# Turning the memory's keys and the compressed branch's weights in 32x32 blocks by way of DRAM

## The chip, the cores and the metric

The kernel runs on one core of one Trainium2 chip. The metric is the time of one execution on the device in microseconds, the median of several runs. A core has five engines with their own instruction queues: TensorE (PE in the profile, with its weight loads as PEld), VectorE (DVE), ScalarE (ACT), GpSimd (POOL) and SyncE (SP). Each queue is worked off in order, and engines wait for each other at semaphores. DMAs are issued from the queues of SP, ACT and POOL.

## The reference, cut to what matters

The kernel computes one decoder block for 512 tokens of width 2048 in float32: a mixer of two head groups (eight NSA heads and four gated linear attention heads), a cross-attention over 256 memory tokens, and a SwiGLU layer. Two places bear on the change.

Each NSA head adds three branches, each an attention over other keys and weighted by a gate. The compressed branch has 31 block keys and values:

```python
s = jnp.einsum('bkgtd,bknd->bkgtn', qb, kc).astype(f32)
...
p = jax.nn.softmax(s, axis=-1)
p = jnp.where(jnp.any(vis, axis=-1)[:, None], p, 0.0)
o_cmp = jnp.einsum('bkgtn,bknd->bkgtd', p.astype(vc.dtype), vc)
...
return gb[..., 0:1] * o_cmp + gb[..., 1:2] * o_slc + gb[..., 2:3] * o_win
```

The cross-attention's keys are made from the memory, normalized by head and scaled by a gain:

```python
ck = rms_norm((hm @ w_ck).reshape(B, M, MEM_HEADS, MEM_DH), g_ck)
s = jnp.einsum('bthd,bmhd->bhtm', cq, ck).astype(jnp.float32)
```

## The kernel before, in words

**Products.** A float32 operand is split into a high part (a ScalarE copy that rounds, line 196) and a rest (a VectorE subtraction, line 196). A product is three matmuls of 512 columns: high by high, high by rest, rest by high (`mm3`, all recorded at line 109). Weights arrive by SP's DMAs, are split into the tiles `wh` and `wl` (three buffers each) and used by `project` and `natural`.

**Order of the work.** The program writes most stages as generators ("flows"). After every few matmuls of a projection the main program calls `flows.tick()`, and each flow whose pause is over adds its next instructions; `yield 2` means a pause of two ticks. A planner then orders each engine's queue by the order of the program, by priorities given to loads, and by modelled durations, and it gives out the tiles' buffers. The order on each queue is fixed before the run.

**The memory's keys.** At the start, `natural`-like loops multiply the memory by `w_cv` and `w_ck`. The flow `mem_keys` computes the norms of the keys and multiplies them in (line 470), which gives two tiles `rows[i]` of 128 memory tokens by 512 (four heads of 128). After a pause of eight ticks, TensorE turns them in eight transposes (line 479) into a PSUM bank `t`, ScalarE scales them by the gain `g_ck` (line 481), and POOL writes them to DRAM (line 440). During the projection by `w_out`, at step m == 4, POOL loads them again (lines 1080 and 1081); at m == 8 they are split into `ckp`, a tile pair with 256 columns for each head.

**An NSA head** (`nsa_head`). The scores of the first branch (selected blocks, with the compressed block scores beside them in the same bank) come first, then `weigh_blocks`: the softmax of the compressed branch in `pc` (128 tokens x 4 token tiles x 32 blocks), and at line 939 its product with the gate's coefficient, written three times side by side into `pc3`. Then come the second branch's scores (window). Later the weights are turned: four transposes of 128x96 (line 982) give `pct`, 96 rows by 512 tokens; ScalarE copies it to `pcs` (line 984) and VectorE replaces rows 64 to 95 by the rests (line 985). For each of the two branches, `turn(j)` transposes the weights (line 994) and splits them, and `weigh(j)` multiplies them by the values into the bank `o`. The first matmul into `o` is the compressed one (`vc` by `pcs`), two ticks after its operand's copy and subtraction. In `vc` rows 0 to 31 are the high part of the compressed values, rows 32 to 63 the rest and rows 64 to 95 the high part again, so that one matmul does all three products. Heads overlap: while one head turns and weighs, the next one computes its scores, and the following projection's matmuls lie between them.

**POOL's queue** also carries sums of later weights made in DRAM (`add_quarters` and `add_block`, lines 154, 156, 169 and 173), each issued after a given matmul; the loads and spills of the gates' rows (lines 1035 and 440, in `swish_gate`, whose product at line 1042 reads the load); and the loads of the mixer's rows (line 1063).

## Time and profile before

| | us |
|---|---|
| median of 3 runs | 2263.38 |
| lowest and highest | 2262.79, 2263.79 |
| the profiled execution | 2262.66 |
| its span, first to last instruction | 2260.9 |
| PE busy | 2252.3 |
| VectorE busy | 1681.7 |
| ScalarE busy | 1154.9 |
| POOL busy | 257.6 |

The profile is of one execution. A group's row gives line, engine, operation, the tile written and those read, the shape, how often, busy time and the mean duration. In a list by time, each row has its start, its length, how many instructions are merged in it, and in brackets how long the engine idled before it and what ended that. Matmuls are pipelined: one starts before the last one has ended, so their durations overlap, and what a matmul costs is the distance between starts. The granted TensorE clock is 1.00 throughout.

### The profile page before, as it was taken

To read this page: it belongs to the slowest core of one execution; us is meant where nothing else is said; L and a number is where in the kernel's file an instruction comes from. 1 tells how busy PE (TensorE), PEld (TensorE's weight loads), DVE (VectorE), ACT (ScalarE), POOL (GpSimd) and SP (SyncE) were. 2 spreads that over 40 slices of the span, in tenths; PEclk is the share of its full clock that TensorE was granted. 3 is DMA by queue.
4 is the path that set the end of the run, shared out by engine and by line. 5 is a ranking of instruction groups with operands and counts; after the bars stand their busy time and mean duration, and the time that the engine had idled before them with its cause. 6 is when DMAs were issued, how large, how long until landed. Compare 5 with 4: busy or idle time off the path is not lost.

```text
span 2260.9 us, 29119 instructions
## 1 busy us (share of the span) xinstructions
PE 2252.3 (100%) x10568; PEld 1871.4 (83%) x10568; DVE 1681.7 (74%) x2547; ACT 1154.9 (51%) x1712; POOL 257.6 (11%) x379
## 2 busy tenths in 40 slices
PE   9999999999999999999999999999999999999999
PEld 7898888888887888888888888888888888888787
DVE  7548876667778435587888888888888887766686
ACT  7534454556677224485455455545554554454443
POOL 0011121111112110020011101101110001001000
PEclk9999999999999999999999999999999999999999
DMA  8587667765558874196466555645564477768675
GB/s 302 176 211 182 166 180 218 208 179 132 163 158 242 219 192 126 56 253 231 140 186 191 167 163 187 192 158 172 190 201 139 155 272 265 266 240 274 244 271 182
DMA packets 129872, 443.59 MB, mean 196 GB/s; under 512 B 15328, under 2 KB 16736, under 8 KB 126784
## 3 DMA queue, kind: packets, MB, share of 16 engines
q1 hardware_dynamic: 83488, 308.97, 40.3%
q0 software_dynamic: 43792, 128.47, 23.5%
q10 hardware_dynamic: 2448, 4.28, 0.5%
q8 instruction: 83, 1.36, 0.2%
q14 instruction: 61, 0.50, 0.1%
HBM read 398.94 MB, written 105.64 MB: 223 GB/s over the span
## 4 chain that ended last, share of the span: by engine, by line
PE 95%; DVE 2%; DMA 2%; issue 1%; ACT 1%; SPq 0%; DVEq 0%; ACTq 0%
PE mm L109 51%; PE t L109 18%; PE s L109 14%; PE o L109 11%; DMA raw<-td 1%; PE t L994 1%; DVE ql L196 1%; DVE wl L196 0%; DMA HR<-h 0%; DMA on<-cmat 0%; DMA PH<-w_ck 0%; ACT wh L196 0%; DVE PB L196 0%; PE t L1151 0%; PE t L982 0%
## 5 line engine op out<-in xcount | busy, mean ns | idle before, releaser
L196 ACT CAST qh<-raw 128x1024 fp32r<-128x1024 f32 (+1 forms) x494 | 477.7, 976 | 453.5 <-PE o L109 131.6
L196 DVE TENSOR_TENSOR ql<-raw,qh 128x1024 fp32r<-128x1024 f32 (+1 forms) x494 | 549.4, 1122 | 81.3 <-PE t L109 25.7
L109 PE MATMUL mm<-X,wh 128*128 128x512 f32 x1664 | 524.1, 395 | 0.0
L109 PEld LDWEIGHTS mm<-X,wh 128*128 128x128 f32 x1664 | 305.7, 188 | 58.5 <-issue 0.8
L109 PE MATMUL t<-qh,PB 128*128 128x512 f32 x968 | 333.1, 389 | 0.0
L109 PE MATMUL mm<-X,wl 128*128 128x512 f32 x832 | 326.6, 393 | 0.2
L196 DVE TENSOR_TENSOR wl<-w,wh 128x1024 fp32r<-128x1024 f32 (+2 forms) x172 | 205.9, 1203 | 158.4 <-ACT wh L196 157.7
L196 ACT CAST wh<-w 128x1024 fp32r<-128x1024 f32 (+2 forms) x172 | 176.5, 1032 | 272.0 <-PE mm L109 181.5
L109 PE MATMUL mm<-qh,PB 128*128 128x512 f32 x868 | 309.3, 390 | 0.0
L109 PE MATMUL s<-qh,PB 128*128 128x512 f32 x672 | 231.1, 389 | 0.0
L109 PE MATMUL mm<-qh,PA 128*128 128x512 f32 x640 | 219.9, 389 | 0.0
L109 PEld LDWEIGHTS t<-qh,PB 128*128 128x128 f32 x968 | 181.7, 188 | 37.7
L109 PEld LDWEIGHTS mm<-qh,PB 128*128 128x128 f32 x868 | 163.0, 188 | 33.8 <-ACT qh L196 0.2
L109 PE MATMUL t<-ql,PB 128*128 128x512 f32 x484 | 188.4, 389 | 0.0
L109 PE MATMUL o<-qh,PB 128*128 128x512 f32 x484 | 187.6, 390 | 0.0
L109 PEld LDWEIGHTS mm<-X,wl 128*128 128x128 f32 x832 | 156.3, 188 | 34.2 <-DVE wl L196 1.7
L109 PE MATMUL mm<-ql,PB 128*128 128x512 f32 x434 | 169.6, 391 | 1.4 <-DVE ql L196 1.3
L109 PEld LDWEIGHTS s<-qh,PB 128*128 128x128 f32 x672 | 126.1, 188 | 25.7
L109 PEld LDWEIGHTS mm<-qh,PA 128*128 128x128 f32 x640 | 120.1, 188 | 24.9
L109 PE MATMUL s<-ql,PB 128*128 128x512 f32 x336 | 131.1, 390 | 0.1
L109 PE MATMUL mm<-ql,PA 128*128 128x512 f32 x320 | 124.6, 389 | 0.0
L1311 DVE TENSOR_TENSOR raw<-raw 128x1024 f32<-128x1024 f32 x80 | 96.9, 1221 | 16.2 <-DMA raw<-w_gu 15.9
(495 smaller groups left out, 3441.3 us busy)
## 6 DMA issues: line engine op xcount, KB each, us to landing
raw<-w_gu SPq DMA_DIRECT2D x80, 768.0 KB, 4.3
raw<-w_down SPq DMA_DIRECT2D x88, 512.0 KB, 5.1
raw<-w_gu SPq DMA_DIRECT2D x80, 512.0 KB, 3.6
td<-w_down POOLq DMA_DIRECT2D x66, 512.0 KB, 7.2
w<-w_a SPq DMA_DIRECT2D x60, 512.0 KB, 5.5
raw<-td SPq DMA_DIRECT2D x22, 1024.0 KB, 6.2
w<-w_out SPq DMA_DIRECT2D x32, 512.0 KB, 4.8
HR<-h POOLq DMA_DIRECT2D x28, 512.0 KB, 5.0
```

Of the source, the lines that this page charges most:

```text
L109: last_mm[0] = PE.matmul(*args, **kw)
L196: last_split[:] = S.copy(hi, src), V.tensor_sub(lo, src, hi)
L994: PE.transpose(tp[:, 128 * (i - j):128 * (i - j) + 128], ps_[b][:, POFF[i] + 128 * j:POFF[i] + 128 * j + 128], ident)
L1311: V.tensor_add(raw[:, 0:1024], raw[:, 0:1024], raw[:, 512:1536])
```

## The change

Both sets of transposes leave TensorE. VectorE turns each 32x32 block in place (`V.transpose`), and the blocks are put in order by the addresses of DMAs to DRAM and back.

The keys: each `rows[i]` is turned into `z`, and four POOL DMAs for each of the two tiles write it to DRAM so that the row is the head's dimension. The gain is applied after loading, at m == 8, by a ScalarE scaling whose input is a strided view; the splits write strided views of `ckp`. The pause of eight ticks becomes two, and there are two ticks after each tile.

The weights: `weigh_blocks` writes the product once into `pw` (128x128), turns it beside itself, writes it to DRAM by one POOL DMA and reads it back three times into `blocks` (96 rows, a buffer of the tag `e`). The copy and the subtraction read `blocks` through strided views, write `pcs` in a buffer of the tag `q1`, and stand with the compressed matmul in `weigh_compressed`, which is called in the second branch after `turn(0)` and its pause. The first matmul into `o` is now the first branch's.

```diff
-        yield 8
-        for a in range(2):
-            tp = bank("t")
-            for h in range(2):
-                for i in range(2):
-                    c = MEM * h + 128 * i
-                    PE.transpose(tp[:, c:c + 128], rows[i][:, 256 * a + 128 * h:256 * a + 128 * h + 128], ident)
-            ck = row("Q")
-            S.activation(ck, tp, AF.Copy, scale=vec("g_ck"))
-            memkv["k", a] = spill(ck)
-            yield 1
+        yield 2
+        for i, t in enumerate(rows):
+            z = row("Q")
+            V.transpose(view(z, 0, (32, 4), (128, 4), (1, 32)), t)
+            d = memkv["k", i] = dram.tile([128, 512], F32, name="ck", tag="ck", bufs=2)
+            for a in range(4):
+                G.dma_start(d[:, 128 * a:128 * a + 128].rearrange("(c s) x -> s c x", s=32),
+                            z[32 * a:32 * a + 32].rearrange("s (c x) -> s c x", x=128))
+            yield 2
...
-            V.tensor_mul(pc3, pc[:, :, None, :].to_broadcast([128, NT, 3, 32]),
-                         cf[:, 0, :][:, :, None, None].to_broadcast([128, NT, 3, 32]))
+            V.tensor_mul(pw[:, :128].rearrange("p (i n) -> p i n", n=32), pc,
+                         cf[:, 0, :][:, :, None].to_broadcast([128, NT, 32]))
+            V.transpose(pw[:, 128:], pw[:, :128])
+            d = dram.tile([128, 128], F32, name="pw", tag="pw", bufs=2)
+            G.dma_start(d, pw[:, 128:])
+            blocks = row("e")[:96]
+            for c in range(3):
+                G.dma_start(blocks[32 * c:32 * c + 32].rearrange("n (a x) -> n a x", x=128),
+                            d.rearrange("(a n) x -> n a x", n=32))
...
-        pct = bank("t")
-        for i in range(NT):
-            PE.transpose(pct[:96, 128 * i:128 * i + 128], pc3[:, i].rearrange("p r n -> p (r n)"), ident)
-        pcs = row("e", F32R)[:96]
-        S.copy(pcs, pct[:96])
-        V.tensor_sub(pcs[64:], pct[64:96], pcs[64:])
         o = None
+
+        def weigh_compressed():
+            pcs = row("q1", F32R)[:96]
+            new, old = [[view(t[a:], 0, *dims) for a in (0, 64)] for t, dims in
+                        ((pcs, ((32, 4), (128, 4), (1, 32))), (blocks, ((128, 4), (32, 4), (1, 32))))]
+            S.copy(new[0], old[0])
+            V.tensor_sub(new[1], old[1], new[1])
+            mm(o, vc[:, 128 * kv:128 * kv + 128], pcs, start=False, stop=False)
+
...
-                    start=False, stop=b == 1 and j == NT - 1)
+                    start=b == 0 and j == 0, stop=b == 1 and j == NT - 1)
...
             if b == 0:
                 o = bank("o")
-                mm(o, vc[:, 128 * kv:128 * kv + 128], pcs, start=True, stop=False)
+            else:
+                weigh_compressed()
...
         if m == 8:
             ckp = sb([128, 1280], "P", 2, F32R), sb([128, 1280], "P", 2, F32R)
-            for a in range(2):
-                split(*part(ckp, 512 * a, 512), ckt[a])
+            for i in range(2):
+                z = row("e")
+                S.activation(view(z, 0, (32, 4), (128, 4), (1, 32)), view(ckt[i], 0, (128, 4), (32, 4), (1, 32)),
+                             AF.Copy, scale=vec("g_ck"))
+                split(*[view(t, 128 * i, (256, 4), (1, 128)) for t in ckp], z.rearrange("p (h n) -> p h n", n=128))
```

## The prediction

> **What bounds the kernel now.** I read the page's busy times and its chain first.

> ```profile
> span 2260.9 us, 29119 instructions
> PE 2252.3 (100%) x10568; PEld 1871.4 (83%) x10568; DVE 1681.7 (74%) x2547; ACT 1154.9 (51%) x1712; POOL 257.6 (11%) x379
> PE 95%; DVE 2%; DMA 2%; issue 1%; ACT 1%; SPq 0%; DVEq 0%; ACTq 0%
> ```

> TensorE is busy for 2252.3 of 2260.9 us and carries 95% of the chain that ended last, so time taken off its queue is time off the end, as long as nothing makes it idle instead. A share over the whole span does not show that for the two stages that change, so next came the table by stretches of time (columns: sum of the stretch, busy PE, PEld, DVE, ACT, POOL with counts, granted clock, DMA share, GB/s). The memory's keys are turned near 62 us, the eight NSA heads run from 412 to 724 us, the turned keys are split between 750 and 800 us.

> ```profile
> 60.00:65.00 5.00, 4.98 (x26) 3.93 (x25) 5.00 (x11) 4.16 (x7) 0.54 (x1) 1.00 0.87 284
> 65.00:70.00 5.00, 5.00 (x23) 4.13 (x22) 4.89 (x9) 5.00 (x9) 0.54 (x1) 1.00 0.96 325
> 80.00:85.00 5.00, 5.00 (x23) 4.13 (x22) 1.82 (x2) 0.82 (x1) 0.00 (x0) 1.00 0.66 210
> 500.00:550.00 50.00, 50.00 (x265) 42.15 (x264) 35.56 (x101) 29.45 (x64) 7.90 (x10) 1.00 0.55 140
> 600.00:650.00 50.00, 50.00 (x267) 42.15 (x266) 36.26 (x108) 34.33 (x76) 8.04 (x11) 1.00 0.61 161
> 650.00:700.00 50.00, 49.66 (x261) 41.22 (x260) 41.08 (x121) 35.50 (x80) 9.69 (x15) 1.00 0.55 151
> 750.00:800.00 50.00, 50.00 (x222) 41.44 (x221) 17.33 (x19) 12.61 (x15) 7.36 (x9) 1.00 0.76 209
> ```

> TensorE has no idle time to give in the heads' stage, at full clock, and VectorE and ScalarE have some 9 us or more of 50 to spare. The list of PE's own waits from 380 to 760 us has one row:

> ```profile
> PE s L109 <- DVE mn L969: 0.3, 1, 0.3
> PEld s L109 <- DVE mn L969: 3.3, 12, 0.8
> ```

> (The second row is of the weight loads' own list, for the same hand-over; loads run ahead of the matmuls.) So both sets of transposes sit in a queue that is full of other matmuls (the next projection fills every gap), and they are paid in full.

> **What is removed.** 40 transposes: 32 of the weights (four for each head, line 982) and 8 of the keys (line 479). Their own rows, then how they stand in time, for head 0 and for the keys:

> ```profile
> L982 PE MATMUL t<-ident,pc x32: 270/273/282, 458.3 to 710.8; 128*96 128x128 f32 x32
> L479 PE MATMUL t<-ident,Q x8: 270/272/327, 62.1 to 64.5; 128*128 128x128 f32 x8
> ...
> 458.28 0.60 PE L982 MATMUL t<-ident,pc 128*96 128x128 f32 x4
> 458.71 0.60 PE L994 MATMUL t<-ident,P 128*128 128x128 f32 x4
> ...
> 62.07 0.83 PE L479 MATMUL t<-ident,Q 128*128 128x128 f32 x4
> 62.35 0.31 PEld L479 LDWEIGHTS t<-ident,Q 128*128 128x128 f32 x3 [0.37 <-DVE Q L470]
> 62.66 0.48 PE L109 MATMUL mm<-wh,X 128*128 128x512 f32 x1
> ```

> One transpose lasts 0.27 us, but four of them are done in 0.60, and the next group starts 0.43 us after the first: 458.71 - 458.28. That is 0.107 us each on the queue. The chain of waits says the same. Its shares for 400 to 725 us and for 55 to 70 us:

> ```profile
> by line: PE mm L109 64.7%; PE o L109 12.8%; PE s L109 11.9%; PE t L994 5.5%; PE t L109 3.8%; PE t L982 1.1%; DVE P L969 0.2%; PE t L831 0.1%; issue 0.0%; DVE mn L969 0.0%
> by line: PE mm L109 71.4%; PE o L109 22.7%; PE t L479 7.3%; issue 0.1%
> ```

> The heads' transposes: 1.1% of 325 us is 3.6 us, against 8 x 0.43 = 3.4 by the timeline; I take 3.5. The keys': 7.3% of 15 us is 1.1 us, with the 0.37 us in it for which the second weight load waited for VectorE's row; that wait goes with the transposes. Without it they are worth 0.7. Taken off: **3.5 + 1.1 = 4.6 us**, bounds 3.4 + 0.7 = 4.1 and 3.6 + 1.1 = 4.7.

> [...]

> **What is added or moved, and what hides it.** The rows that price it:

> ```profile
> L984 ACT CAST e<-t x8: 576/579/586, 458.9 to 711.4; 96x512 fp32r<-96x512 f32 x8
> L985 DVE TENSOR_TENSOR e<-t,e x8: 689/689/690, 459.5 to 712.2; 32x512 fp32r<-32x512 f32 x8
> L939 DVE TENSOR_TENSOR pc<-pc,cf x8: 549/550/559, 413.8 to 694.7; 128x384 f32<-128x384 f32 x8
> L935 DVE TENSOR_TENSOR pc<-pc,qs x8: 279/288/292, 412.0 to 690.7; 128x128 f32<-128x128 f32 x8
> L481 ACT ACTIVATE Q<-t,vecs x2: 674/677/680, 63.4 to 65.2; 128x512 f32<-128x512 f32 x2
> L1429 DVE STREAM_TRANSPOSE HR<-HR 128x512 f32<-128x512 f32 x16 | 10.5, 690 | 0.2 <-DMA HR<-x 0.2
> ```

> VectorE, heads: the product shrinks from 128x384 (0.55 us) to 128x128 (0.29), and a 128x128 turn comes in, a quarter of the 128x512 turn's 0.69, 0.17. The difference is under 0.1 us a head. VectorE, keys: two turns, 1.4 us, at 62 us, where it is full (5.00 of 5). What covers it: from 80 to 85 us VectorE works 1.82 of 5, and weight tiles are split three deep, so the 1.4 us are taken up before PE runs out of weights; without that cover they would cost 1.4. ScalarE: the two scalings of 0.68 leave that stage and come back between 750 and 800 us, where it works 12.61 of 50. The shorter pause of the key flow (2 ticks, not 8) moves work forward into VectorE's full stretch and nothing on PE. The product with the block values stays one 512-column matmul; it only moves to the second branch.

> The heads' ScalarE copy (L984) and VectorE subtraction (L985) stay, at 0.58 and 0.69 us if reading SBUF costs what reading PSUM did. But they move: before, two ticks of other matmuls lay between them and the product that reads them; now copy, subtraction and product stand together, and behind the product in the same PSUM bank wait the first value products of the second branch. **This is the unknown of the change.** Bounds a head: 0, if PE has other matmuls placed there, and 0.58 + 0.69 = 1.27, if it stands still for both; over eight heads 0 to 10.2 us. The nearest row is the hand-over of the scores' bank from VectorE to PE, which has no pause either: its weight loads waited twelve times, 3.3 us in all, and the matmuls for 0.3 us of that. Eight of twelve make 0.2 us, and I take that, near the lower end.

> The round trip through DRAM: POOL issues one write and three reads a head (32 more in all, of 64 KB), and eight writes for two with the keys (6 more). The reads wait on POOL for the write to land. Queued behind them on POOL: the sums in DRAM (L154, L156, L169, L173), the loads of the gates' rows (L1035), the spills. Rows for its length, head 2 and head 7:

> ```profile
> POOL gu L173 <- PE mm L109: 24.9, 3, 10.5
> gu<-w_gu POOLq DMA_DIRECT2D x8, 512.0 KB, 9.2
> x2r<-HR POOLq DMA_DIRECT2D x32, 128.0 KB, 2.6
> DMA to landing us min/median/max: 3.5/5.7/6.5
> ...
> 524.57 0.55 DVE L939 TENSOR_TENSOR pc<-pc,cf 128x384 f32<-128x384 f32 x1
> 559.28 0.48 PE L109 MATMUL o<-PH,KV 128*128 128x512 f32 x1
> 694.68 0.55 DVE L939 TENSOR_TENSOR pc<-pc,cf 128x384 f32<-128x384 f32 x1
> 719.75 0.50 PE L109 MATMUL o<-PH,KV 128*128 128x512 f32 x1
> ```

> The weights are made at 525.1 and 695.2; the first product that must come after them in the new place is at 559.3 and 719.7: 34 and 24.5 us of room. The trip takes 2 x 2.6 = 5.2 us at best, 2 x (9.2 + 10.5) = 39 at worst (two landings of the slowest kind, two sums waiting for PE ahead of it). By the nearest row, the 256 KB loads' 5.7 us, with one wait of 8, it is 19: hidden, cost 0.

> The sum: 4.6 - 0.2 = 4.4 us. The profiled execution took 2262.66 us around its span of 2260.9; the median of the three runs is 2263.38, 0.7 above. 2263.38 - 4.4 = **2259.0 us**, 0.19% less. About 0.2%, or 4.5 us, is what a measurement of this kernel can tell from no change, so the forecast lies on that edge.

> **The rivals.**

> *The transposes cost their duration.* 40 x 0.272 = 10.9 us go, or any part of the difference to 4.6 through freed PSUM banks: 2252.5 to 2258. For it: the duration rows. Against: the start times, and that PE waits for no bank now.

> *POOL's queue is held by the landings.* The tightest load behind it:

> ```profile
> 493.48 1.21 POOL L154 DMA_DIRECT2D td<-td  x1 [7.19 <-DMA w<-w_a]
> 494.22 1.08 POOL L1035 DMA_DIRECT2D st<-spill  x1
> L1042 DVE TENSOR_TENSOR st<-st,q x8: 679/691/692, 500.3 to 710.3; 128x512 f32<-128x512 f32 x8
> ```

> Issued at 494.2, landed 5.7 later, read at 500.3: 0.4 us to spare. Two landings, 11.4 us, less the 7.2 that POOL idles there anyway, make VectorE stand for up to 3.8 us, with PE's weights behind it; weights split ahead cover part of that. Half of that, at this gate and again at the last one, is 3.8 us lost: 2262.8. [...]

> *Another limit takes the gain.* The span stays, 2263.4. Against it: the 9 us and more that VectorE has free in each 50.

> *Slower: the product stands in PE's way.* The place is the second branch of every head, where PE's queue order is fixed before the run. If copy and subtraction come later than that order assumes, PE stops. From 4.5 / 8 = 0.56 us a head on, the gain is gone; at the full 1.27 it is 10.2 - 4.6 = 5.6 us slower, 2269.0. For it: no pause is left between them. Against it: the 0.3 us of PE's list.

> **How the numbers follow.** Forecast 0.62 (2257.5 to 2260.3), 0.29 below the 0.2% edge at 2258.85 and 0.33 above it; duration rival 0.09, faster; POOL 0.14 and another limit 0.05, no change; slower 0.10. Faster: 0.29 + 0.09 = 0.38. Same: 0.33 + 0.14 + 0.05 = 0.52. Slower: 0.10. The range leaves out most of the slower case and the deep part of the duration case: 2256.8 to 2263.4.

> **What would show it.** Lines 982 and 479 gone, PE's busy time down by 4 to 5 us, its head's period shorter by 0.43 us, and still no PE wait on the weights' tile in the heads' stage. Wrong it is if PE waits for ScalarE's or VectorE's part of the new product, if ScalarE waits for the read from DRAM, or if the gates' product waits for its load.

## The result, and the profile after

The changed kernel takes 2279.9 us (median of 6 runs, 2277.6 to 2282.9), the kernel before on the same chip 2263.1 (6 runs, 2262.3 to 2264.3): ratio 1.0073, 95% interval 1.0062 to 1.0083. By the ratio it is slower by 16.5 us (by the medians 16.8), where 4.4 us less were forecast. The profiled execution took 2281.3 us. All ratios here compare undisturbed executions; one execution of the run e7 below took 3516.3 us at a mean granted clock of 0.60 and is left out of its ratio.

The page of the kernel after, its busy times and its chain by line:

```profile
span 2279.5 us, 29129 instructions
PE 2254.8 (99%) x10528; PEld 1870.8 (82%) x10528; DVE 1683.0 (74%) x2557; ACT 1156.5 (51%) x1712; POOL 279.0 (12%) x417
PE mm L109 37%; PE t L109 15%; PE s L109 12%; PE o L109 8%; DMA e<-pw 1%; PE t L1004 1%; DMA st<-ck 0%; DMA raw<-gu 0%; DMA HR<-h 0%; ACT wh L196 0%; DVE ql L196 0%; DMA ss<-KV 0%; PE t L1165 0%; POOL e L946 0%; ACT e L1151 0%
```

The forty transposes are gone (10528 PE instructions instead of 10568), yet the span is 18.6 us longer and PE is busy 2.5 us *more*. The chain now runs through DMAs that were not on it before: `e<-pw`, the weights' read from DRAM, `st<-ck`, the keys' load (the kernel before loads them too, but off the chain), and through POOL's issue of the reads (`e L946`).

Where the time went is read from instructions that both kernels have. First the kernel before, from its lists by line (count, shortest, median and longest duration in ns, first and last start in us): the transposes of the compressed keys and values (the first ahead of the heads, the last in head 0) and those of the cross-attention; then the windows of the two stretches in question (columns as in the prediction).

```profile
L831 PE MATMUL t<-ident,q x4: 222/248/272, 362.2 to 454.6; 64*128 64x64 f32 x4
L1151 PE MATMUL t<-ident,e x32: 270/273/332, 907.9 to 954.8; 128*128 128x128 f32 x32
...
380.00:760.00 380.00, 379.63 (x1940) 316.07 (x1939) 262.86 (x694) 232.03 (x480) 66.58 (x89) 1.00 0.68 185
2060.00:2165.00 105.00, 103.66 (x457) 85.11 (x456) 74.68 (x76) 47.68 (x49) 9.09 (x17) 1.00 0.76 267
```

The same of the kernel after:

```profile
L829 PE MATMUL t<-ident,q x4: 222/248/272, 361.1 to 457.4; 64*128 64x64 f32 x4
L1165 PE MATMUL t<-ident,e x32: 270/273/328, 921.5 to 968.4; 128*128 128x128 f32 x32
...
380.00:760.00 380.00, 366.83 (x1843) 304.12 (x1842) 258.11 (x697) 230.51 (x478) 81.58 (x117) 0.99 0.68 184
2060.00:2165.00 105.00, 102.06 (x441) 83.49 (x440) 69.20 (x66) 49.90 (x51) 10.16 (x19) 0.98 0.69 250
```

Ahead of the heads the new kernel leads by 1.1 us (361.1 against 362.2): the keys' part does what was forecast. After head 0 it is 2.8 us behind (457.4 against 454.6), after the heads 13.6 (921.5 against 907.9), at the end 18.6. So 14.7 us are lost between 361 and 908, and 5.0 behind it. In the heads' stage TensorE idles for 13.2 us where it idled for 0.4, and its granted clock falls to 0.99.

PE's three largest waits ahead of 900 us in the kernel after name three places, and the waits of ScalarE and VectorE from 400 to 740 us say what stands behind the first:

```profile
PE s L109 <- DVE mn L976: 7.7, 3, 3.2
PE o L109 <- ACT PH L196: 3.0, 1, 3.0
...
PE mm L109 <- DVE wl L196: 2.2, 1, 2.2
...
ACT q L993 <- DMA e<-pw: 11.9, 3, 4.6
...
DVE q L994 <- ACT q L993: 9.5, 3, 3.8
```

**Heads 2, 3 and 4 (7.7 us).** The timeline around head 2, all engines:

```profile
526.66 0.31 DVE L941 STREAM_TRANSPOSE pw<-pw 128x128 f32<-128x128 f32 x1
527.27 0.62 POOL L943 DMA_DIRECT2D pw<-pw  x1 [4.23 <-DVE pw L941]
530.39 1.67 POOL L946 DMA_DIRECT2D e<-pw  x3 [2.50 <-issue]
531.86 0.63 ACT L1051 ACTIVATE st<-st 128x512 f32<-128x512 f32 x1
536.10 0.62 ACT L993 CAST q<-e 96x512 fp32r<-96x512 f32 x1 [3.60 <-DMA e<-pw]
536.62 1.30 ACT L964 ACTIVATE P<-cm,qs 128x128 f32<-128x128 f32 x3
537.82 1.50 PE L109 MATMUL s<-KV,Q 128*128 128x384 f32 x6 [2.23 <-DVE mn L976]
```

The turned weights leave at 527.3 and are back at 536.1, 9.1 us after the turn's end at 527.0. The product that needs them comes only at 562.8. But ScalarE's copy of them (line 993) stands in ScalarE's queue right behind the gate's instruction of line 1051, 27 us ahead of that product, and holds everything behind it for 3.6 us. Next behind it is line 964, which prepares the next score tiles; VectorE's reduction of the scores (line 976) needs that, and PE's next scores need the bank which the reduction gives back. In the kernel before, ScalarE's queue had the same neighbours and nothing between them; the copy from PSUM (line 984) came later, with its operand there and no wait:

```profile
529.86 0.63 ACT L1040 ACTIVATE st<-st 128x512 f32<-128x512 f32 x1
532.58 1.31 ACT L957 ACTIVATE P<-cm,qs 128x128 f32<-128x128 f32 x3 [2.09 <-PE t L994]
...
537.85 0.58 ACT L984 CAST e<-t 96x512 fp32r<-96x512 f32 x1
```

**The keys (3.0 us).** The same at the end of the stage, kernel after:

```profile
714.64 0.54 POOL L1091 DMA_DIRECT2D st<-ck  x1
722.86 0.72 ACT L1097 ACTIVATE e<-st,vecs 128x512 f32<-128x512 f32 x1 [2.86 <-DMA st<-ck]
724.59 0.79 PE L109 MATMUL o<-PH,KV 128*128 128x512 f32 x1 [3.00 <-ACT PH L196]
```

The keys' scaling (line 1097) stands ahead of the cast that the last head's value product needs, and waits for a load that takes 8.2 us from issue to landing.

**Head 0 (2.2 us)** is another thing. POOL and the engines behind it, kernel after:

```profile
412.81 0.61 POOL L943 DMA_DIRECT2D pw<-pw  x1 [1.82 <-DVE pw L941]
417.94 1.66 POOL L946 DMA_DIRECT2D e<-pw  x3 [4.51 <-DMA pw<-pw]
420.32 1.03 POOL L786 MEMSET e<- 128x512 f32 x1
421.39 0.58 DVE L792 TENSOR_TENSOR e<-KV,vecs 128x248 f32<-128x248 f32 x1 [3.79 <-POOL e L786]
423.16 0.50 PE L109 MATMUL mm<-wl,X 128*128 128x512 f32 x1 [2.15 <-DVE wl L196]
```

POOL waits 4.5 us for the write to land before it may issue the reads, so its memset (line 786, zeros for the blocks of the compressed values) starts at 420.3. VectorE waits for that, and the rests of the projection's weights stand behind it.

**The clock.** The windows behind two of these stops, and behind one with no effect (PE's clock is the first number of the last three):

```profile
423.70:427.10 3.40, 3.40 (x9) 2.67 (x8) 2.91 (x7) 1.01 (x3) 0.57 (x1) 0.50 1.02 195
537.80:541.20 3.40, 3.38 (x15) 2.84 (x16) 1.58 (x8) 3.15 (x10) 0.70 (x1) 1.00 0.03 7
611.40:614.80 3.40, 3.02 (x8) 2.63 (x9) 1.89 (x10) 2.62 (x8) 0.00 (x0) 0.51 0.15 61
```

For 3.4 us PE runs at half clock; that is up to 1.7 us of work each time, and PE counts as busy in it. It came after head 0, head 4, the keys and a stop at 2151.8. At head 4 and at the keys the slow stretch begins 0.3 and 0.5 us before the stop ends, so there it costs 1.5 us, and the three together 4.7. Added up from 361 to 908: TensorE idles 12.8 us more than before (the three stops are 12.9, and the kernel before had one of 0.3), which makes 17.5 with the clock's 4.7; less the 14.7 lost leaves 2.8 that the missing transposes gave, where 3.5 were forecast. Two runs below (e8, e12) give 2.5 to 2.6.

### The profile page after: what moved, and what is told of

It is laid out like the page before. It is cut to its first block, busy times and chain, and to the rows that moved or that the text cites. A ratio compares the mean times of both kernels' runs of the same rounds, so it can differ in the third digit from the quotient of the medians.

```text
span 2279.5 us, 29129 instructions
## 1 busy us (share of the span) xinstructions
PE 2254.8 (99%) x10528; PEld 1870.8 (82%) x10528; DVE 1683.0 (74%) x2557; ACT 1156.5 (51%) x1712; POOL 279.0 (12%) x417
## 4 chain that ended last, share of the span: by engine, by line
PE 73%; DMA 2%; DVE 1%; ACT 1%; issue 0%; POOL 0%; ACTq 0%; DVEq 0%; SPq 0%; POOLq 0%
PE mm L109 37%; PE t L109 15%; PE s L109 12%; PE o L109 8%; DMA e<-pw 1%; PE t L1004 1%; DMA st<-ck 0%; DMA raw<-gu 0%; DMA HR<-h 0%; ACT wh L196 0%; DVE ql L196 0%; DMA ss<-KV 0%; PE t L1165 0%; POOL e L946 0%; ACT e L1151 0%
## 5 line engine op out<-in xcount | busy, mean ns | idle before, releaser
L109 PE MATMUL mm<-X,wh 128*128 128x512 f32 x1664 | 524.1, 395 | 0.2 <-ACT X L196 0.2
L109 PEld LDWEIGHTS mm<-X,wh 128*128 128x128 f32 x1664 | 305.7, 188 | 59.0 <-ACT X L196 1.0
L109 PE MATMUL t<-qh,PB 128*128 128x512 f32 x968 | 333.0, 389 | 0.0
L109 PE MATMUL mm<-X,wl 128*128 128x512 f32 x832 | 326.6, 393 | 0.2
L109 PE MATMUL mm<-qh,PB 128*128 128x512 f32 x868 | 309.6, 390 | 0.7 <-ACT qh L196 0.7
L109 PE MATMUL s<-qh,PB 128*128 128x512 f32 x672 | 231.0, 389 | 0.0
L109 PE MATMUL mm<-qh,PA 128*128 128x512 f32 x640 | 219.8, 389 | 0.0
L109 PEld LDWEIGHTS t<-qh,PB 128*128 128x128 f32 x968 | 181.8, 188 | 38.0
L109 PEld LDWEIGHTS mm<-qh,PB 128*128 128x128 f32 x868 | 163.1, 188 | 34.9 <-ACT qh L196 1.3
L109 PE MATMUL t<-ql,PB 128*128 128x512 f32 x484 | 188.3, 389 | 0.0
L109 PE MATMUL o<-qh,PB 128*128 128x512 f32 x484 | 188.2, 391 | 0.0
L109 PEld LDWEIGHTS mm<-X,wl 128*128 128x128 f32 x832 | 156.7, 188 | 34.7 <-DVE wl L196 1.7
L109 PE MATMUL mm<-ql,PB 128*128 128x512 f32 x434 | 169.9, 391 | 2.4 <-DVE ql L196 2.3
L109 PEld LDWEIGHTS s<-qh,PB 128*128 128x128 f32 x672 | 126.2, 188 | 25.9
L109 PEld LDWEIGHTS mm<-qh,PA 128*128 128x128 f32 x640 | 120.1, 188 | 25.1
L109 PE MATMUL s<-ql,PB 128*128 128x512 f32 x336 | 131.2, 390 | 0.9 <-DVE ql L196 0.9
L109 PE MATMUL mm<-ql,PA 128*128 128x512 f32 x320 | 124.5, 389 | 0.0
## 6 DMA issues: line engine op xcount, KB each, us to landing
raw<-w_down SPq DMA_DIRECT2D x88, 512.0 KB, 4.9
raw<-w_gu SPq DMA_DIRECT2D x80, 512.0 KB, 3.6
td<-w_down POOLq DMA_DIRECT2D x66, 512.0 KB, 7.1
w<-w_a SPq DMA_DIRECT2D x60, 512.0 KB, 5.3
w<-w_out SPq DMA_DIRECT2D x32, 512.0 KB, 4.7
HR<-h POOLq DMA_DIRECT2D x28, 512.0 KB, 4.6
```

The source lines that it names most:

```text
L109: last_mm[0] = PE.matmul(*args, **kw)
```

## The experiments

Theory A, from the trace: instructions that read DMA data were placed in ScalarE's fixed order for an earlier landing than they get, and POOL's memset stands behind a landing. Theory B, the slower rival of the prediction: copy, subtraction and product stand together without a pause and hold PE. Theory C: POOL's queue, held by the landings, delays other loads.

The offset in this table is the start of the cross-attention's transposes in each kernel's profiled execution, less the 907.9 us of the kernel before: what was won or lost up to there, in one execution each. The change is the ratio's, in us of 2263, with its 95% interval.

| kernel | offset at 908 us | ratio | change at the end |
|---|---|---|---|
| after | +13.6 | 1.0073 | +16.5 (+14.0 to +18.8) |
| e1, keys' part alone | +0.6 | 1.0012 | +2.7 (+0.5 to +5.0) |
| e2, weights' part alone | +11.0 | 1.0068 | +15.4 (+10.4 to +20.6) |
| e3, copy placed late | +8.9 | 1.0062 | +14.0 (+10.6 to +17.4) |
| e5, and keys' scaling late | -1.3 | 1.0025 | +5.7 (+3.6 to +7.7) |
| e6, and memset on VectorE | -2.7 | 1.0004 | +0.9 (-1.1 to +2.9) |
| e7, keys' part alone, scaling late | -1.2 | 0.9998 | -0.5 (-2.7 to +1.6) |
| e10, weights' part alone, late, memset on VectorE | +2.2 | 1.0014 | +3.2 (+1.1 to +5.2) |
| e9, before, with an unread round trip | +5.4 | 1.0026 | +5.9 (+3.6 to +8.1) |
| e4, before, 40 transposes doubled | +6.1 | 1.0031 | +7.0 (+4.1 to +10.0) |
| e8, before, 32 transposes left out | -2.5 | 0.9998 | -0.5 (-2.5 to +1.4) |
| e12, the same again | -2.6 | 0.9993 | -1.6 (-3.6 to +0.2) |
| e11, before, 128 transposes left out | -11.6 | 0.9940 | -13.6 (-16.5 to -10.6) |

### e1 and e2: one part alone

```diff
 e1: before.py with the hunks of mem_keys and of m == 8 alone
 e2: before.py with the hunks of nsa_head (pw, weigh_compressed) alone
```

> The keys' part of the change alone; the weights are turned by TensorE as before. Theory A (ScalarE instructions that read a DMA's data are placed in ScalarE's queue too early for the real landing, and everything behind them waits): the scaling of the loaded keys stands near 717 us with its load still under way, as in the changed kernel, where TensorE then lost 3.2 + 0.7 us and 1.7 us by a halved clock; less 1.1 us for the keys' transposes: 2263.1 + 4.5 = about 2267.6. Theory B (the chain of copy, subtraction and product in the heads is the loss) and theory C (POOL's queue, held by the weights' round trip, is the loss): neither is in this kernel, so 2263.1 - 1.1 = 2262.0.

> The weights' part alone; the keys are turned by TensorE as before. Theory A: the stalls of heads 0 and 2 to 4 stay (2.3 + 2.4 + 2.4 + 3.4 us, twice 1.7 us by the clock), those of the keys' scaling go, 3.5 us of transposes are saved: about 2263.1 + 10.5 + 3.4 - 3.5 = 2273.5. Theories B and C: the whole loss is here, 2279.9 + 1.1 = about 2281.

By the times the weights' part carries nearly the whole loss: e2's +15.4 lies between theory A's +10.4 us and the 18 of B and C and decides nothing by itself; e1's +2.7 fits A's 4.5 and not the gain of 1.1 that B and C expected. The traces say more. The main wait of PE in e2 and ScalarE's wait on a DMA, from 380 to 760 us, then PE's one wait in the keys' part (e1) with ScalarE's:

```profile
PE s L109 <- DVE mn L978: 7.2, 3, 3.8
...
ACT q L995 <- DMA e<-pw: 11.3, 3, 5.1
```

```profile
PE o L109 <- ACT PH L196: 2.1, 1, 2.1
...
ACT st L196 <- DMA st<-spill: 1.8, 1, 1.8
```

The stops of heads 2 and 4 come back in e2 at full length. In e1 there is a stop at 720 us as well, but one instruction group on: the keys' scaling finds its data there, and the split of the memory's *values*, next in the program, waits for its load. The keys' part wins 1.4 us at the start and loses 2.1 here.

### e3, e5, e6: the same work, placed later

The arguments in the code are shortened (`...`). `behind` makes the instructions in its block stand behind the named ones in their engines' queues. e3 puts copy and subtraction behind the second branch's first split, e5 also the keys' scaling and splits (and with them what follows) behind the sum of squares of the step before, e6 also moves head 0's memset to VectorE. Nothing else changes.

```diff
 e3, e5, e6 (weigh_compressed):
-            S.copy(new[0], old[0])
-            V.tensor_sub(new[1], old[1], new[1])
+            with behind(*turned_1):            # turned_1: the split of turn(0)
+                S.copy(new[0], old[0])
+                V.tensor_sub(new[1], old[1], new[1])
 e5, e6 (m == 8):
+                with behind(*squared):         # squared: Square and its sum at m == 7
                     S.activation(view(z, ...), view(ckt[i], ...), AF.Copy, scale=vec("g_ck"))
                     split(...)
 e6 (compress_blocks):
-        G.memset(blk, 0.0)
+        (V if pe == "pe_v" else G).memset(blk, 0.0)
```

> The changed kernel with the copy and the subtraction of the weights kept behind the split of the second branch's first turn on their own engines' queues, some 20 us later; their chain to the product and POOL's DMAs stay. Theory A: the stalls of heads 2 to 4 go, 2.4 + 2.4 + 3.4 us and one halved clock of 1.7: 2279.9 - 9.9 = about 2270. Theory B: no pause is added, so 2280 or slower. Theory C: POOL's queue is the same, so 2280.

> The copy kept back as in the run before (e3), and also the scaling and the splits of the loaded keys kept behind the sum of squares of the column tile before them. Theory A: TensorE's stop near 716 us (5.8 us in e3, with two halved-clock stretches of 1.7 us each) goes; what stays is the stop of head 0 (2.4 us and one halved clock): the median of the kernel before + 2.4 + 1.7 - 4.6 plus what the down-projection loses more, 1 to 3 us: 0 to 3 us slower than before. Theory B (chain of copy, subtraction and product): still there, as slow as e3, some 13 us above before. Theory C (POOL's queue): the same, some 13 us above before.

> As e5, and the clearing of the compressed values' blocks moves from POOL, where it stood behind the wait for the first write of head 0's weights, to VectorE. Theory A with the one place where POOL's queue counts: no stop of TensorE is left between 60 and 1000 us beyond those of the kernel before, and the 40 transposes are gone: 4 to 5 us faster than the kernel before (ratio 0.998), if the stops near 1030 and 2140 us are the chip's and not the change's; 0 to 2 us faster if they are the change's. Theories B and C: slower than before by 8 us or more.

PE's waits from 380 to 760 us; e3 with ScalarE's on DMAs, then e5, then e6:

```profile
PE o L109 <- ACT PH L196: 5.4, 1, 5.4
PE mm L109 <- DVE wl L196: 2.0, 1, 2.0
...
ACT e L1099 <- DMA st<-ck: 4.6, 1, 4.6
```

```profile
PE mm L109 <- DVE wl L196: 1.9, 1, 1.9
```

```profile
PE o L109 <- DVE q L995: 0.4, 1, 0.4
```

Each step removes the wait it aims at and no other. In e3 the 7.7 us of heads 2 to 4 are gone, but PE reaches the keys' place earlier, their load does not, and that stop grows from 3.0 to 5.4 us with 6.8 us of half clock: the end gains only 2.5 of 16.5 us, where theory A had expected 9.9. By its time alone e3 would fit B and C better; the waits decide. e5 removes that, 8.3 us by the ratios; e6 removes head 0's, 4.8 us. Of the 16.5 us of loss 15.6 follow from three places in the queues' order, with the round trip, the copies and the product kept. Two expectations were still too hopeful: e5 was to be 0 to 3 us slower and is 5.7 slower, and e6 was to be faster by up to 5 us and cannot be told from no change. In e6 copy, subtraction and product still stand together, and PE waits 0.4 us for them in all: theory B falls.

The profiled execution of e5 was the fastest of its ten (2263.9 us, median 2269.4), so its offset is lower than in most of them. Its stop at head 0 (PE's wait 1.9 us) left the clock at 1.00; at the same place 2.0 us in e3 and 2.2 us in the kernel after were followed by 0.50, 2.0 us in e2 were not. The last section shows how these stops lay. That the other executions of e5 lose their 5 us in this way was not seen, as only one was profiled.

### e7: the keys' part, placed late

```diff
 e1 with the hunk of e5 at m == 8
```

> The keys' part alone (as e1), with the scaling and splits kept back. Theory A: the stop near 720 us (2.5 us in e1) goes and the keys' transposes are saved: 1.1 us faster than before. If the stop in e1 had another cause than the scaling's place, it stays: 1 to 2 us slower than before, as e1.

The stop at 720 us is gone (PE is busy for all 15.0 us from 715 to 730; in e1 for 12.9), and the lead of 1.2 us holds to 908 us. At the end it cannot be told from no change, nor from the 1.1 us that were expected.

### e4, e8, e12, e11: what the transposes are worth

The arguments of e4's transposes are shortened (`...`); its second hunk doubles those of line 982 in the same way.

```diff
 e4:
-                    PE.transpose(tp[:, c:c + 128], ...)
+                    for _ in range(2):
+                      PE.transpose(tp[:, c:c + 128], ...)
 e8, e12:
-        pct = bank("t")
-        for i in range(NT):
-            PE.transpose(pct[:96, 128 * i:128 * i + 128], pc3[:, i].rearrange("p r n -> p (r n)"), ident)
         pcs = row("e", F32R)[:96]
-        S.copy(pcs, pct[:96])
-        V.tensor_sub(pcs[64:], pct[64:96], pcs[64:])
+        pv = pcs.rearrange("p (i r n) -> p i r n", r=4, n=32)
+        S.copy(pv, pc3[:96, :, 0:1, :].to_broadcast([96, NT, 4, 32]))
+        V.tensor_sub(pv[64:], pc3[64:96, :, 0:1, :].to_broadcast([32, NT, 4, 32]), pv[64:])
 e11, as e8 and:
             def turn(j):
+                if j:
+                    split(*part(pt, TOFF[j], n), ps_[b][:, TOFF[j]:TOFF[j] + n])
+                    return
```

> The kernel before with each of the 40 transposes done twice into the same place: the price of 40 transposes on TensorE's queue. By the distance of starts (0.107 us) with no wait in it: 40 x 0.107 = 4.3 us more, about 2267.4. By the duration of 0.272 us: 10.9 more, 2274. If they were hidden: 2263.1.

> The kernel before without the 32 transposes of the weights: ScalarE's copy and VectorE's subtraction read the weights' own tile in the same shapes, so the product gets numbers that are not turned, and the output is not the reference's. Nothing else is taken away, and no transfer is added. By the distance of starts (0.107 us each) the time falls by 3.4 to 3.6 us, ratio 0.9985, and the heads' stage is shorter by as much. If the transposes are worth only what the run with everything pinned won in the heads' stage (1.5 us), the ratio is 0.9993. By their duration, 32 x 0.272 = 8.7 us, it would be 0.996.

> The kernel without the weights' 32 transposes once more, beside the run with 128 fewer on the same chip: 2.5 us below the kernel before (ratio 0.9989) if the gain of the heads' stage comes through to the end; no difference (1.0000) if the last stage takes it back.

> The kernel before without the 32 transposes of the weights and without 96 of the 160 transposes of the two branches' scores (all but those of the first column block); the splits read the scores' own tile in the same shapes, so the products get numbers that are not turned and the output is not the reference's. 128 transposes fewer. If what is taken off TensorE's queue ahead of 725 us comes off the end one for one, the time falls by 128 x 0.107 = 13.7 us by the distance of starts, or by 128 x 0.08 = 10 us by what the run without the weights' transposes won inside the heads' stage (2.5 us for 32): ratio 0.994 to 0.9956. If the end is held by something later than the heads (the loads ahead of the last products near 2120 us), the heads' stage is shorter by 10 to 14 us and the end by 3 us less or more than that: ratio 0.997 and above. By their duration it would be 35 us, 0.985.

The transposes of the cross-attention in e8 and in e11 (before: from 907.9 on; e12: from 905.3):

```profile
L1149 PE MATMUL t<-ident,e x32: 270/273/332, 905.4 to 952.3; 128*128 128x128 f32 x32
```

```profile
L1152 PE MATMUL t<-ident,e x32: 270/273/332, 896.3 to 943.2; 128*128 128x128 f32 x32
```

Without the 32 transposes, and with nothing added, the heads' stage is 2.5 to 2.6 us shorter, 0.08 us each. At the end the two runs give -0.5 and -1.6 us, on average -1, with intervals that hold both 0 and -2.5. With 128 fewer the end comes 13.6 us earlier, 0.106 us each (0.083 to 0.129 by the interval); by their duration it would have been 35. So gains ahead of 725 us do reach the end, the distance of starts (0.107) is about the right price, and the duration rival is out. The exact agreement is luck: e11's 11.6 us at 908 us hold a stop and a halved clock, shown next, of 3.9 us together, and without them the stage would give 15.5, 0.121 each.

Doubling in e4 came out between the two prices: 7.0 us (4.1 to 10.0), where the distance of starts gives 4.3 and the duration 10.9. In its trace the keys' sixteen transposes carry 11.6% of the chain from 55 to 70 us, 1.74 us, 0.109 each with any wait among them. PE's waits from 380 to 760 us are 1.4 us there instead of 0.3, most of them for VectorE's rests of the weights (`PL`), and at the end 3.4 us of half clock between 2060 and 2165 us (mean clock 0.98) come on top; what the rest of the +6.1 at 908 us is was not found. In these profiled executions a transpose added cost 0.15 us (6.1 for 40), and one left out gave back 0.08 (2.5 for 32).

What reaches the end of 2.5 us is below what ten to twenty runs of this kernel tell.

e11 shows theory A's mechanism in work that the change never touched. ScalarE's wait on a DMA and PE's wait, from 380 to 760 us:

```profile
PE mm L109 <- ACT X L196: 2.2, 1, 2.2
...
ACT P L196 <- DMA st<-spill: 4.0, 1, 4.0
```

This is the split of the old keys, which TensorE turned. With PE 11 us earlier, their load is late, ScalarE's queue stands for 4.0 us, PE for 2.2, and the clock is halved for 3.4 us.

### e9: the round trip that nobody reads

```diff
 before.py, in weigh_blocks behind the product into pc3:
+            d = dram.tile([128, 128], F32, name="pw", tag="pw", bufs=2)
+            G.dma_start(d, pc.rearrange("p i n -> p (i n)"))
+            blocks = row("e")[:96]
+            for c in range(3):
+                G.dma_start(blocks[32 * c:32 * c + 32].rearrange("n (a x) -> n a x", x=128),
+                            d.rearrange("(a n) x -> n a x", n=32))
```

> The kernel before with a DRAM round trip a head added that nobody reads: one 64 KB write of the 128x128 weights and three dependent reads on POOL's queue, at the place of the change. The transposes stay. If what the detour costs is only the early place of the instructions that read it, then all that remains here is head 0, where POOL's later memset is held behind the reads' issue: one stop of some 2.5 us of TensorE with or without a halved clock, +2 to +4 us, ratio 1.001 to 1.002, and no stop at the later heads. If the transfers themselves disturb (POOL's queue, the weights' loads), there are stops at every head and more losses near 1030 us, and the ratio is 1.004 or more.

Timeline of POOL and VectorE at head 0, then PE's waits from 380 to 760 us:

```profile
418.59 1.79 POOL L945 DMA_DIRECT2D e<-pw  x3 [5.64 <-DMA pw<-pc]
422.22 0.52 POOL L788 MEMSET e<- 128x512 f32 x1
...
420.94 0.59 DVE L794 TENSOR_TENSOR e<-KV,vecs 128x248 f32<-128x248 f32 x1 [4.99 <-POOL e L788]
...
PE mm L109 <- ACT wh L196: 2.6, 1, 2.6
```

One stop at head 0, with half clock behind it (mean clock 0.97 from 400 to 450 us), and none at the later heads: the offset is +5.4 us, nearly all of it from head 0, and the end moves by 5.9 (3.6 to 8.1), where 2 to 4 us were expected of a single stop. PE waits 3.1 us in all from 380 to 760 us, 2.6 of them for this stop: the transfers alone disturb next to nothing else there, so theory C holds for head 0 and for nothing after it; and the stops at heads 2 to 4 need the reader.

### e10: the weights' part alone, placed late

```diff
 e2 with the hunks of e3 and e6
```

> The weights' part alone, the keys as before, with the copy and the subtraction put behind the second branch's first split and the memset of head 0 on VectorE. No stop is left in the heads' stage. If that were all that the detour costs, the time would fall by the worth of the 32 transposes, 3.5 us, ratio 0.9985. If the detour has a cost that doesn't hang on where its readers are put, it stays at the before time or above: the run with everything pinned was 1.3 us above, the keys alone pinned 0.6 below, and the difference, 1.9 us, makes a ratio of 1.0008.

Expected was a stage without a stop; there was one, at head 7. ScalarE's timeline there:

```profile
718.91 0.62 ACT L196 CAST P<-st 128x512 fp32r<-128x512 f32 x1 [2.79 <-DMA st<-spill]
```

It is the split of the keys again, in their old form as in e11, 2.2 us for PE and 3.4 us of half clock (1.7 us lost). Without both the offset would be 2.2 - 3.9 = -1.7. e6 less e7 says the same of the weights' part, -2.7 + 1.2 = -1.5. So with its stops taken out the detour wins 1.5 to 1.7 us in the heads' stage, where leaving the turn out altogether wins 2.5, and at the end that does not show.

## Why the prediction was wrong

**The transposes taken off, 4.6 us.** The way of pricing them was right, distance of starts and not duration: 0.08 us each in e8 and e12, 0.106 in e11 (0.083 to 0.129), where the prediction said 0.107. The keys' 1.1 us came as 1.1 in the kernel after, 1.2 in e7. Of the weights' 3.5 us the heads' stage shows 2.5 to 2.6; this term was 1 us too high for what a stage without any stop gives back.

**VectorE's turns hidden, and the prices of copy and subtraction.** Right. The turn of the weights takes 0.31 us, not a quarter of 0.69; no engine but POOL, which issues its write, waits for it. The copy costs 0.62 us from SBUF, 0.58 from PSUM; the subtraction 0.68 and 0.69.

**"The unknown of the change", 0.2 us.** The chain of copy, subtraction and product was near nothing, as taken: 0.4 us in e6, where it is alone. The prediction looked for the danger here and put its slower rival on it. That rival had the right sign and the wrong place: in the kernel after PE never stopped for the product, and the loss was three times what the rival gave at its worst.

**"34 and 24.5 us of room … hidden, cost 0": this step failed.** The trip itself came out shorter than the 19 us estimated. Turn to landing was 9.1 us in head 2, 7.3 to 10.1 over the eight heads. But the room was measured to the *product*. The first instruction that reads the data is ScalarE's copy; the order of its queue is fixed before the run, and the copy was put 27 us ahead of the product. In head 2 ScalarE comes to it at 532.5 (531.86 + 0.63), 5.5 us behind the turn's end at 527.0. Against 5.5 us of room a trip of 9.1 is not hidden, and what waits is not the copy alone but every instruction behind it on ScalarE: 7.7 us of PE in three heads. The prediction named the sign, "if ScalarE waits for the read from DRAM", but gave it no price, though nothing in the diff holds the copy back until its data are there.

**The keys' scaling, "where it works 12.61 of 50".** The same mistake, on top of a wrong reading: the turned keys are not split between 750 and 800 us. In the kernel before, ScalarE splits them at 717.9, while the heads are still at work:

```profile
717.91 1.14 ACT L196 CAST P<-st 128x512 fp32r<-128x512 f32 x2
```

From 700 to 750 us ScalarE works 33.61 of 50. Their first load was issued at 705.1, 12.8 us ahead of this split. In the kernel after ScalarE comes to the scaling at 720.0, 5.4 us behind the load's issue at 714.64. So the scaling began only at 722.9; it stands ahead of a cast that the last head needed, and it cost 3.0 us and a halved clock; in e3, with PE earlier, 5.4 us and twice the time at half clock.

**"POOL's queue is held by the landings".** The mechanism was right, at head 0. The prediction listed the loads and sums queued behind the reads and left out the memset of line 786, which is no DMA. It cost 3.9 us in the kernel after (from 1.1 ahead to 2.8 behind), and in e9 by itself 5.9 at the end; the prediction gave this rival 3.8. No gate's load waited.

**Behind 908 us.** 5.0 us more are lost there in the profiled execution of the kernel after, most of them near 2140 us, where the windows above show PE at 0.98 of its clock. The order of every engine's instructions in that stretch is the same in all kernels here, so the difference is one of times and not of order, probably of when data arrive; that was not shown. PE's waits from 2060 us on are 1.3 us in the profile of the kernel before, 1.3 in e7, 3.0 in the kernel after, 3.1 in e8 and 4.6 in e6, with 3.4 us of half clock in the kernel after and e8 and 6.8 in e6, and with no clear relation to the offset at 908. Whether the small gains of e6 to e8 and e12 are lost there or only lie within the scatter stays open.

## What to carry to other kernels

When an operand comes to an engine by DMA instead of by an engine, measure the room to the *first instruction that reads it in its engine's fixed queue*, not to the result's use, and ask what is queued behind that reader; then place the reader late by hand. Ask also what is queued behind a wait for a write to land: here POOL waited 4.5 us for its own write, and VectorE stood 3.8 us for the memset queued behind it. In this kernel, whose main engine has no idle time, such a stop (PE's wait 2.2 and 3.0 us in the kernel after) cost up to 1.7 us more in clock, and the one of 5.4 us in e3 up to 3.4; and saving time ahead of a load moved the same stop to the next load that was just in time (ScalarE's waits for it: 1.8 us in e1, 4.6 in e3, 2.8 in e10, 4.0 in e11).

## What the runs showed of the hardware that was not expected

In the kernel after, the stops can be told apart by where they lie on a fixed grid. The stretches at full clock between two at half clock last 184.3, 109.2 and 1426.8 us there, which is 54, 32 and 418 times 3413.3 ns. So this execution can be cut into steps of 3413 ns, and TensorE's idle time counted in each. From 20 us after the start of the span to 15 us before its end, the four steps at full clock with the most idle time, 2.08, 2.15, 2.48 and 2.90 us, were followed by half clock; the next two, with 1.85 and 1.47 us, were not. The stop at head 0 in two kernels, e2 and then e3 (PE's wait 2.0 us in both), each in two such steps (idle is the first number less PE's busy time):

```profile
419.95:423.37 3.42, 2.26 (x16) 1.76 (x14) 0.89 (x2) 2.63 (x3) 2.50 (x4) 1.00 0.39 73
423.37:426.78 3.41, 2.53 (x11) 2.11 (x12) 3.41 (x5) 0.00 (x0) 0.57 (x1) 1.00 1.09 180
...
419.68:423.10 3.42, 1.38 (x10) 1.01 (x9) 2.12 (x3) 1.39 (x2) 1.26 (x2) 1.00 0.67 95
423.10:426.51 3.41, 3.41 (x10) 2.64 (x9) 3.03 (x6) 0.84 (x3) 0.57 (x1) 0.50 1.04 207
```

In e2 these steps cut the stop into 1.16 and 0.88 us, and the clock of the second step is 1.00; in e3 2.04 us fall into one step, and the next is at 0.50. So the same stop was followed by a loss of up to 1.7 us in the one profiled execution and by none in the other.

A load of 256 KB issued on POOL's queue at 714.6 took 8.2 us to land, where the gates' loads of this size had a median of 5.7 in the kernel before. From 700 to 750 us the kernel before shows its DMA engines at a share of 1.01, against 0.55 to 0.82 in the 300 us ahead. The keys' load came late there in four kernels (after, e3, e10, e11), in two different forms, and the values' load in e1.
